# Sending the products of the recurrence's gates and of the pooling's groups as 272, 264 and 256 columns, with their sample sums joined

## The chip, the cores and the metric

The kernel runs on one core of a Trainium2 chip. Its engines work side by side and wait for each other only where one needs what another makes: PE multiplies matrices into accumulators, DVE and ACT do elementwise work (ACT also the sigmoids and exponentials), POOL does a little more of it, and SP starts the transfers. Every engine takes its instructions in the order in which they are written. The metric is the time of one execution on the device, in microseconds (us).

## The reference

One layer of a decoder is computed for 256 prompt tokens and 8 sample tokens (264 columns in the kernel), in float32 with a model width of 2048:

```python
xn = rms_norm(x, g_mix)
z = xn @ w_in                       # u_pool 512 | u_lru 1024 | u_gel 1024 | c_a 512 | c_b 512
y_pool = pool_mixer(u_pool, ...)    # trailing means less the token, then 4 blocks 128x128, a scale
xc = causal_dwconv(u_lru, 4 taps)
gate_r = sigmoid(xc_block @ w_a + b_a)      # 8 blocks of 128x128
gate_i = sigmoid(xc_block @ w_x + b_x)      # 8 blocks of 128x128
a = exp(-8 * gate_r * softplus(-lam))
h = scan(a, xc * gate_i * sqrt(1 - a*a))
y_lru = (h * gelu(u_gel)) @ w_lru_br
y_conf = silu(layer_norm(causal_dwconv(c_a * sigmoid(c_b), 31 taps))) @ w_conf_br
x = x + (sum of sigmoid(xn @ w_gate + b_gate) * (y_pool @ w_pool_br, y_lru, y_conf)) @ w_out
x = x + square(relu(rms_norm(x, g_mlp) @ w_up)) @ w_down
y = rms_norm(x, g_final)
```

The states of the convolutions, of the pooling and of the recurrence come back as further outputs. The change touches the sixteen products that make `gate_r` and `gate_i`, and the four 128x128 products of the pooling's groups.

## The kernel before, in words

The work lies transposed: channels on the 128 partitions, the 264 tokens in the columns. Each float32 number is held as two parts in a shorter format, a high part (the number rounded) and a low part (the rest). A product is the sum of three: high weight times high token, low weight times high token, high weight times low token; low times low is left out. Tokens lie in memory as low part (columns 0 to 263) and then high part (264 to 527), each with the 256 prompt tokens ahead of the 8 samples.

There are two forms of the three products, in `mm3` and `mm` (from line 238):

```python
ALIKE = (False, N, 2 * N), (True, N, 2 * N), (False, 0, N)
MIXED = (False, TP, 2 * N), (True, N, 2 * N), (False, 0, TP)
```

ALIKE sends 264 columns three times, and all land on the accumulator's columns 8 to 271. MIXED sends 272 columns (the low parts of the 8 samples and all high parts, which lie side by side), 264, and 256 (the low parts of the prompt). Both are 792 columns. In MIXED the low parts of the samples land apart, in columns 0 to 7, and have to be added to the samples' columns afterwards. `join` (lines 159 to 166) does that: one engine, ACT or DVE, copies the 8 columns to a small tile `side`, and DVE adds them to the accumulator. The dense products use MIXED, and `join` (or an addition in their evacuation) follows them at the end of each group. The sixteen gate products and the four pooling products use ALIKE and need no join.

The weights come as a stream of chunks, 1024 columns wide (eight 128x128 blocks, 24 matmuls, each with its weight load) or 512 for the gates and the groups (12 matmuls). For each chunk ACT rounds it to its high part `whi` (line 222) and DVE takes the difference for the low part `wlo` (line 223). There are four buffers for each, and the split of the chunk three places ahead is written out ahead of the matmuls of the chunk at hand. Eight chunks make a dense group of four accumulators; there are eight accumulators in all (`bufs=8`), so an open group leaves four free.

The gate products stand in four chunks of 512 columns, called gate blocks one to four below, put behind chunks 1, 3, 5 and 6 of the dense group w_in 4 (`LRU_AT`, line 55). So between blocks one and two, and two and three, stand two dense chunks, between three and four one, and behind block four the last chunk of that group; then the next group (w_in 6) opens with four accumulators. Each block makes two channel tiles of two gates, in the four accumulators that the open group leaves free. ACT reads each with a sigmoid (lines 525 and 526), and with that the accumulator is free for the next block, or for the next group. The pooling's groups take one such chunk in the middle of group w_gate 0; ACT reads their four accumulators at line 779.

The order on each engine is that of the main loop (from line 1008): in each turn the split of the chunk three ahead, the matmuls, the evacuation of a finished group, then the background work of the three mixers as far as a planner's credits allow: for DVE here the pooling's running sums (line 745) and differences (lines 757 to 762), and the product with the second gate (line 530). Those instructions stay in that order on the chip, whatever is ready.

Of the kernel before, what the change touches and what calls it, by code (L numbers as in the profile page):

```python
# [92 lines left out]
def hybrid_step(ctx: ExitStack, tc: tile.TileContext, first, par_in, st_in, wall, y_out, st_out):  # L93
# [17 lines left out]
    L = cpool.tile([P, 8 * PITCH], F32R, name="L", tag="L")  # L111
# [10 lines left out]
    def pv(name, i=None, n=1):  # L122
        a, b = PCOL[name]
        return par[:, a:b] if i is None else par[:, a + i:a + i + n]

    def part(t, k, a, n):
        at = k * PITCH + SKEW + a
        return t[:, at:at + n]
# [7 lines left out]
    def both(t, k):  # L136
        return part(t, k, 0, 2 * N)
# [4 lines left out]
    def lows(t, k):  # L142
        return two_of(t, k, 0)

    def highs(t, k):
        return two_of(t, k, N)
# [4 lines left out]
    def acc():  # L151
        return psum.tile([P, 512], F32, name="acc", tag="acc")

    def tokens(ps):
        return ps[:, TS:TS + N]
# [3 lines left out]
    def join(ps, by_act):  # L159
        t = side[:, len(joined) % 4, :]  # L160
        joined.append(t)
        if by_act:
            nc.scalar.copy(t, ps[:, :TS])
        else:
            nc.vector.tensor_copy(t, ps[:, :TS])
        nc.vector.tensor_tensor(ps[:, N:N + TS], ps[:, N:N + TS], t, op=ALU.add)
# [71 lines left out]
    ALIKE = (False, N, 2 * N), (True, N, 2 * N), (False, 0, N)  # L238
    MIXED = (False, TP, 2 * N), (True, N, 2 * N), (False, 0, TP)
# [6 lines left out]
    def mm(ps, hi, lo, x, what, start, stop=False):  # L246
        low_w, a, b = what
        o = TS + N - (b - a) if b > N else TS
        nc.tensor.matmul(ps[:, o:o + b - a], lo if low_w else hi, x[:, a:b], start=start, stop=stop,  # L249
                         skip_group_check=True)  # L250

    def mm3(ps, hi, lo, x, first, last, form):
        for k in range(3):
            mm(ps, hi, lo, x, form[k], first and k == 0, last and k == 2)
# [16 lines left out]
    def mark(q, flag):  # L271
        stage(q, "none", 0.0, [lambda: done.add(flag)], 0)

    def later(n, fn):
        delayed.append((now[0] + n, fn))
# [26 lines left out]
    def spend(**kw):  # L302
        for e, c in kw.items():
            credit[e] -= c
# [205 lines left out]
    def stage_split(q, n, hi, lo, x, gap=1):  # L510

        stage(q, "act", 0.65, [lambda i=i: nc.scalar.copy(hi(i), x(i)) for i in range(n)])
        stage(q, "dve", 0.71, [lambda i=i: nc.vector.tensor_tensor(lo(i), x(i), f(hi(i)), op=ALU.subtract)
                               for i in range(n)], gap)

    def lru_gate_mm(ct, c, j):
        assert "xc" in done
        hi, lo = whi[:, c % NHI, :], wlo[:, c % NHI, :]
        out = []
        for t in range(2):  # L520
            s = slice((2 * j + t) * P, (2 * j + t + 1) * P)
            ps = acc()
            mm3(ps, hi[:, s], lo[:, s], both(L, ct), True, True, ALIKE)
            out.append(ps)
        nc.scalar.activation(RA[:, ct, :], tokens(out[0]), AF.Sigmoid, bias=pv("b_lru_a", ct))
        nc.scalar.activation(TM[:, ct, :], tokens(out[1]), AF.Sigmoid, bias=pv("b_lru_x", ct))
        spend(act=1.0)
        if ct % 2:
            def times():
                nc.vector.tensor_tensor(XC[:, ct - 1:ct + 1, :], XC[:, ct - 1:ct + 1, :], TM[:, ct - 1:ct + 1, :],  # L530
                                        op=ALU.mult)
                spend(dve=0.71)

            later(1, times)
# [198 lines left out]
    def Q():  # L733
        if not q_at:
            q_at.append(cpool.tile([P, 8 * PITCH], F32R, name="Q", tag="Q"))
        return q_at[0]
# [35 lines left out]
    def grp_mm(c):  # L772
        assert "pool" in done
        hi, lo = whi[:, c % NHI, :], wlo[:, c % NHI, :]
        for gi in range(4):
            s = slice(gi * P, (gi + 1) * P)
            ps = acc()
            mm3(ps, hi[:, s], lo[:, s], both(Q(), gi), True, True, ALIKE)
            nc.scalar.activation(DU[:, gi, :], tokens(ps), AF.Copy, scale=pv("pool_scale", gi))
        stage_split("pool", 2, lambda c: highs(Q(), 2 * c), lambda c: lows(Q(), 2 * c), lambda c: DU[:, 2 * c:2 * c + 2, :])  # L780
        mark("pool", "grp")
# [226 lines left out]
    for i, ch in enumerate(chunks):  # L1008
# [18 lines left out]
        kind, gi, c, _ = ch  # L1027
# [26 lines left out]
        elif kind == "lru":  # L1054
            for j in range(2):
                lru_gate_mm(2 * gi + j, i, j)
            if gi == 3:
                lru_tail()
        elif kind == "grp":
            grp_mm(i)  # L1060
# [198 lines left out]
```

## Time and profile before

| | us |
|---|---|
| median of three runs (lowest, highest) | 1372.77 (1372.33, 1373.48) |
| the profiled execution | 1372.8 |
| its span on the core | 1370.9 |
| PE busy | 1365.0 |
| DVE busy | 894.3 |
| ACT busy | 729.4 |
| gate blocks one to four on PE | 102.5 to 122.6 |
| pooling's groups on PE | 182.6 to 184.0 |

A row of the timeline gives start, duration, engine, line and operation, the tile written and the tiles read, the shape, how many were merged into the row, and in brackets how long the engine stood idle ahead of it and for whom. Durations of neighbours on one engine overlap by about a tenth of a microsecond, since an instruction starts while the one ahead of it is still writing; so a place in a queue is priced by the distance of two starts.

### The profile page before, as it was taken

The page shows a single profiled execution, that of the slowest core. Times are in us where ns is not written, and L with a number is a line of the kernel's source. Part 1 is how long each engine was busy: PE and PEld are TensorE (multiplying, and loading weights), DVE is VectorE, ACT ScalarE, POOL GpSimd, SP SyncE. Part 2 cuts the span into 40 slices and gives each one's busy share as a digit, 9 for nine tenths or more (in the row PEclk, how much of TensorE's full clock was granted, in tenths as well). Part 3 has the DMA queues.
Part 4 walks back from the last instruction along what each step waited for, and adds up shares of the span by engine and source line. Part 5 has one row for each costly group of instructions (what it writes and reads, how often), then busy time and mean ns, then how long its engine had stood idle before and what let it go on. Part 6 is the DMA issues. An engine that isn't in the chain of part 4 may idle for free.

```text
span 1370.9 us, 27000 instructions
## 1 busy us (share of the span) xinstructions
PE 1365.0 (100%) x11459; PEld 1363.4 (99%) x11459; DVE 894.3 (65%) x1470; ACT 729.4 (53%) x1067; POOL 88.0 (6%) x122
## 2 busy tenths in 40 slices
PE   9999999999999999999999999999999999999998
PEld 9999999999999999999999999999999999999998
DVE  8777888876877669666656455655465645465644
ACT  7667677657664646455544334543344533354544
POOL 0300010110102014011000000000000000000112
PEclk9999999999999999999999999999999999999999
DMA  8655555555565555555555555555555555555552
GB/s 322 213 188 188 182 192 192 184 182 189 186 209 191 183 185 173 197 182 184 189 185 185 185 185 185 186 184 185 184 186 185 185 185 185 185 186 185 183 187 85
DMA packets 40968, 257.51 MB, mean 188 GB/s; under 512 B 4496, under 2 KB 6672, under 8 KB 11920
## 3 DMA queue, kind: packets, MB, share of 16 engines
q1 hardware_dynamic: 40704, 255.67, 55.0%
q8 instruction: 89, 1.46, 0.4%
q14 instruction: 31, 0.25, 0.1%
q10 hardware_dynamic: 144, 0.13, 0.0%
HBM read 252.57 MB, written 3.21 MB: 187 GB/s over the span
## 4 chain that ended last, share of the span: by engine, by line
PE 99%; DVE 0%; issue 0%; DVEq 0%
PE acc L249 99%; PE acc L346 0%; DVE y L1119 0%; DVE G L1114 0%; DVE X L900 0%; PE acc L329 0%; DVE G L1131 0%; DVE y L1153 0%; DVE G L902 0%; DVE G L1110 0%; DVE G L1113 0%; DVE X L911 0%; DVE X L906 0%; DVE G L1112 0%; DVEq L1153 0%
## 5 line engine op out<-in xcount | busy, mean ns | idle before, releaser
L223 DVE TENSOR_TENSOR wlo<-raw,whi 128x1024 fp32r<-128x1024 f32 (+1 forms) x478 | 581.5, 1219 | 435.2 <-ACT whi L222 434.6
L222 ACT CAST whi<-raw 128x1024 fp32r<-128x1024 f32 (+1 forms) x478 | 496.9, 1042 | 568.7 <-PE acc L249 500.5
L249 PE MATMUL acc<-A,whi 128*128 128x272 f32 (+2 forms) x3968 | 708.1, 282 | 0.0
L249 PEld LDWEIGHTS acc<-A,whi 128*128 128x128 f32 x3968 | 609.2, 188 | 0.5 <-ACT whi L232 0.5
L249 PE MATMUL acc<-A,wlo 128*128 128x264 f32 x1984 | 555.7, 282 | 0.0
L249 PEld LDWEIGHTS acc<-A,wlo 128*128 128x128 f32 x1984 | 371.0, 188 | 0.0
L249 PE MATMUL acc<-xn,whi 128*128 128x272 f32 (+1 forms) x2048 | 365.6, 281 | 0.0
L249 PEld LDWEIGHTS acc<-xn,whi 128*128 128x128 f32 x2048 | 314.6, 188 | 0.0
L249 PE MATMUL acc<-xn,wlo 128*128 128x264 f32 x1024 | 288.7, 282 | 0.0
L249 PEld LDWEIGHTS acc<-xn,wlo 128*128 128x128 f32 x1024 | 192.3, 188 | 0.0
L249 PE MATMUL acc<-Q,whi 128*128 128x256 f32 (+2 forms) x776 | 140.7, 281 | 0.0
L249 PE MATMUL acc<-LH,whi 128*128 128x272 f32 (+1 forms) x768 | 138.7, 281 | 0.0
L249 PEld LDWEIGHTS acc<-Q,whi 128*128 128x128 f32 x776 | 120.1, 188 | 0.0
L249 PEld LDWEIGHTS acc<-LH,whi 128*128 128x128 f32 x768 | 118.6, 188 | 0.0
L249 PE MATMUL acc<-Q,wlo 128*128 128x264 f32 x388 | 109.5, 282 | 0.0
L249 PE MATMUL acc<-LH,wlo 128*128 128x264 f32 x384 | 108.2, 282 | 0.0
L249 PEld LDWEIGHTS acc<-Q,wlo 128*128 128x128 f32 x388 | 72.9, 188 | 0.0
L249 PEld LDWEIGHTS acc<-LH,wlo 128*128 128x128 f32 x384 | 72.1, 188 | 0.0
L646 ACT ACTIVATE G<-tmp,par 128x256 f32<-128x256 f32 x120 | 54.4, 500 | 8.4 <-DVE G L649 7.5
L924 POOL TENSOR_SCALAR G<-G 128x264 f32<-128x264 f32 x1 | 0.4, 418 | 656.8 <-ACT G L866 656.8
L649 DVE TENSOR_TENSOR G<-G 128x1024 f32<-128x1024 f32 x30 | 38.2, 1274 | 0.0
L914 DVE TENSOR_TENSOR X<-X,acc 128x264 f32<-128x264 f32 x79 | 33.5, 424 | 6.4 <-PE acc L249 6.4
(193 smaller groups left out, 622.9 us busy)
## 6 DMA issues: line engine op xcount, KB each, us to landing
raw<-wall_dram SPq DMA_DIRECT2D x226, 1024.0 KB, 4.9
raw<-wall_dram SPq DMA_DIRECT2D x12, 512.0 KB, 6.1
raw<-first_dram SPq DMA_DIRECT2D x6, 512.0 KB, 8.2
y_dram<-y SPq DMA_DIRECT2D x7, 256.0 KB, 2.4
X<-first_dram SPq DMA_DIRECT2D x6, 264.0 KB, 7.9
raw<-wall_dram SPq DMA_DIRECT2D x5, 256.0 KB, 3.2
tmp<-first_dram SPq DMA_DIRECT2D x3, 388.0 KB, 5.0
tmp<-st_dram SPq DMA_DIRECT2D x4, 188.0 KB, 5.1
```

Of the source, the lines that this page charges most:

```text
L222: nc.scalar.copy(h[:, s], r[:, s])
L223: nc.vector.tensor_tensor(lo[:, s], r[:, s], f(h[:, s]), op=ALU.subtract)
L249: nc.tensor.matmul(ps[:, o:o + b - a], lo if low_w else hi, x[:, a:b], start=start, stop=stop, skip_group_check=True)
L646: nc.scalar.activation(dst[:, ct, :TP], vext[:, ct, k:k + TP], AF.Copy, scale=par[:, w:w + 1])
L649: nc.vector.tensor_tensor(VC[:, :, :TP], VC[:, :, :TP], src[:, :, :TP], op=ALU.add)
L914: nc.vector.tensor_tensor(X[:, m, :], X[:, m, :], tokens(whole), op=ALU.add)
L924: nc.gpsimd.tensor_scalar(sq2, sq2, 1.0, EPS * D / P, op0=ALU.mult, op1=ALU.add)
```

## The change

The gate products and the pooling's products take the form MIXED, and each is followed at once by `join`. In a pair of gates the first is copied by ACT and the second by DVE; of the four pooling groups, 0 and 2 by ACT and 1 and 3 by DVE. No matmul is added or taken away.

```diff
@@ lru_gate_mm
         for t in range(2):
             s = slice((2 * j + t) * P, (2 * j + t + 1) * P)
             ps = acc()
-            mm3(ps, hi[:, s], lo[:, s], both(L, ct), True, True, ALIKE)
+            mm3(ps, hi[:, s], lo[:, s], both(L, ct), True, True, MIXED)
+            join(ps, t == 0)
             out.append(ps)
         nc.scalar.activation(RA[:, ct, :], tokens(out[0]), AF.Sigmoid, bias=pv("b_lru_a", ct))
         nc.scalar.activation(TM[:, ct, :], tokens(out[1]), AF.Sigmoid, bias=pv("b_lru_x", ct))
@@ grp_mm
-            mm3(ps, hi[:, s], lo[:, s], both(Q(), gi), True, True, ALIKE)
+            mm3(ps, hi[:, s], lo[:, s], both(Q(), gi), True, True, MIXED)
+            join(ps, gi % 2 == 0)
             nc.scalar.activation(DU[:, gi, :], tokens(ps), AF.Copy, scale=pv("pool_scale", gi))
```

Three places show what it does to the order. The first is DVE's queue around gate block four, before: `L223` are splits of weight chunks, `L530` multiplies by the second gate, `L513` splits the pooling's differences, and `acc_1224` belongs to the dense group that ends there.

```order
L223 TENSOR_TENSOR wlo_65<-raw_63,whi_64 128x1024 x2
L530 TENSOR_TENSOR G_76<-G_76,tmp0_69 128x528
L513 TENSOR_TENSOR Q_1482<-G_76,Q_1482 128x2x264 x2
L223 TENSOR_TENSOR wlo_65<-raw_63,whi_64 128x1024 x2
L166 TENSOR_TENSOR acc_1224<-acc_1224,side_83 128x8
```

The same queue now, with the accumulators 1541 to 1561 of gate block four:

```order
L223 TENSOR_TENSOR wlo_65<-raw_63,whi_64 128x1024
L531 TENSOR_TENSOR G_76<-G_76,tmp0_69 128x528
L513 TENSOR_TENSOR Q_1506<-G_76,Q_1506 128x2x264 x2
L223 TENSOR_TENSOR wlo_65<-raw_63,whi_64 128x1024
L166 TENSOR_TENSOR acc_1541<-acc_1541,side_83 128x8
L165 COPY side_83<-acc_1547 128x8
L166 TENSOR_TENSOR acc_1547<-acc_1547,side_83 128x8
L166 TENSOR_TENSOR acc_1555<-acc_1555,side_83 128x8
L165 COPY side_83<-acc_1561 128x8
L166 TENSOR_TENSOR acc_1561<-acc_1561,side_83 128x8
L223 TENSOR_TENSOR wlo_65<-raw_63,whi_64 128x1024
L166 TENSOR_TENSOR acc_1224<-acc_1224,side_83 128x8
```

DVE, which had no part in the gates' accumulators, now has six small instructions there (four additions, two copies), behind two splits of weight chunks and the other work of those turns.

The second place is ACT's queue at the same block, before (`L546` is the tanh that opens the recurrence's tail):

```order
L512 CAST Q_1482<-G_76 128x2x264 x2
L222 CAST whi_64<-raw_63 128x1024 x2
L525 ACTIVATE tmp2_71<-acc_1517,par_66 128x264
L526 ACTIVATE tmp0_69<-acc_1521,par_66 128x264
L525 ACTIVATE tmp2_71<-acc_1527,par_66 128x264
L526 ACTIVATE tmp0_69<-acc_1531,par_66 128x264
L546 ACTIVATE tmp0_69<-tmp2_71,sp_81 128x264 x3
```

And now:

```order
L512 CAST Q_1506<-G_76 128x2x264 x2
L222 CAST whi_64<-raw_63 128x1024 x2
L163 COPY side_83<-acc_1541 128x8
L526 ACTIVATE tmp2_71<-acc_1541,par_66 128x264
L527 ACTIVATE tmp0_69<-acc_1547,par_66 128x264
L163 COPY side_83<-acc_1555 128x8
L526 ACTIVATE tmp2_71<-acc_1555,par_66 128x264
L527 ACTIVATE tmp0_69<-acc_1561,par_66 128x264
L547 ACTIVATE tmp0_69<-tmp2_71,sp_81 128x264 x3
```

Ahead of each pair of sigmoids stands a copy, and the second pair's copy stands behind the first pair's sigmoids. Each sigmoid now reads what DVE's addition has written.

The third place is PE's queue where the next dense group (w_in 6) opens, now, with what each matmul waits for:

```order
L249 MATMUL acc_1227<-A_68,whi_64 128x256
L249 MATMUL acc_1617<-A_68,whi_64 128x272 [waits Activation_49]
L249 MATMUL acc_1617<-A_68,wlo_65 128x264
L249 MATMUL acc_1617<-A_68,whi_64 128x256
L249 MATMUL acc_1618<-A_68,whi_64 128x272 [waits Activation_49]
L249 MATMUL acc_1618<-A_68,wlo_65 128x264
L249 MATMUL acc_1618<-A_68,whi_64 128x256
L249 MATMUL acc_1619<-A_68,whi_64 128x272 [waits Activation_49]
```

These accumulators are the places of block four's, 1541 to 1561, in the same order, and the waits for ACT are for its sigmoids; before, the same four places were handed on in the same way. Gate blocks two to four take the places of the block ahead of them.

## The prediction

> **What bounds the kernel now.** I read the page's busy shares and its chain of waits, then the stretch of the gate blocks by windows, then the timeline of each engine there.
>
> ```profile
> span 1370.9 us, 27000 instructions
> PE 1365.0 (100%) x11459; PEld 1363.4 (99%) x11459; DVE 894.3 (65%) x1470; ACT 729.4 (53%) x1067; POOL 88.0 (6%) x122
> ...
> PE 99%; DVE 0%; issue 0%; DVEq 0%
> ```
>
> PE never pauses and is 99% of the chain that ends last. So every time at which PE has to wait is added to the end, and work elsewhere costs nothing until PE waits for it. The stretch of the four gate blocks (engines in the order PE, PEld, DVE, ACT, POOL):
>
> ```profile
> 102.50:126.00 23.50, 23.50 (x199) 23.50 (x198) 19.24 (x39) 17.01 (x31) 0.00 (x0) 1.00 0.57 189
> ```
>
> PE has no gap there, and DVE is busy for 19.24 of 23.50 us (82%), against 65% over the span: it is the engine with the least room, and the one that the change adds to. PE's places:
>
> ```profile
> 121.19 0.28 PE L249 MATMUL acc<-L,whi 128*128 128x264 f32 x1
> ...
> 122.65 0.28 PE L249 MATMUL acc<-A,whi 128*128 128x272 f32 x1
> ...
> 125.39 0.41 PE L249 MATMUL acc<-A,whi 128*128 128x256 f32 x2
> ...
> 189.63 0.41 PE L249 MATMUL acc<-A,whi 128*128 128x256 f32 x2
> ```
>
> Block four starts at 121.19, the last dense chunk at 122.65. The second of the two matmuls merged at 125.39 opens the next dense group, at 125.51. At 189.63 the second likewise opens the second chunk behind the pooling's groups (189.75).
>
> **What the columns are worth.** Both forms send 792 columns for a product. Twelve ALIKE matmuls take 122.65 - 121.19 = 1.46 us, 0.1217 each; 24 MIXED ones take 125.51 - 122.65 = 2.86, 0.1192 each. Sixty matmuls change: at most 60 x 0.0025 = 0.15 gained; I take -0.13. The Trainium skill, TensorE: Matmul & The Clock Gate, section Back-to-back issue gap, gives for matmuls in a row a fixed cost and a rate per column, by which three matmuls of 792 columns cost the same however they are cut; the sum by it would be 0.13 higher. The rows differ from it slightly, and they decide.
>
> **What a join costs where it stands.** Twenty additions and ten copies go to DVE, ten copies to ACT:
>
> ```profile
> L163 ACT COPY side<-acc 128x8 f32<-128x8 f32 x44 | 6.7, 170 | 12.4 <-PE acc L249 12.4
> ...
> 127.38 0.17 DVE L166 TENSOR_TENSOR acc<-acc,side 128x8 f32<-128x8 f32 x1
> 127.58 0.43 DVE L596 TENSOR_TENSOR tmp<-acc,rstd 128x264 f32<-128x264 f32 x1
> ```
>
> And ACT's rows at the blocks, where before DVE had no part:
>
> ```profile
> 103.24 0.48 ACT L525 ACTIVATE tmp<-acc,par 128x264 f32<-128x264 f32 x1
> ...
> 104.70 1.07 ACT L222 CAST whi<-raw 128x1024 fp32r<-128x1024 f32 x1
> ...
> 119.48 1.18 ACT L512 CAST Q<-G 128x528 fp32r<-128x528 f32 x2
> 120.54 2.02 ACT L222 CAST whi<-raw 128x1024 fp32r<-128x1024 f32 x2
> ...
> 123.53 0.52 ACT L526 ACTIVATE tmp<-acc,par 128x264 f32<-128x264 f32 x1
> 123.90 1.37 ACT L546 ACTIVATE tmp<-tmp,sp 128x264 f32<-128x264 f32 x3
> 125.12 1.09 ACT L222 CAST whi<-raw 128x1024 fp32r<-128x1024 f32 x1
> ...
> 130.37 0.92 ACT L546 ACTIVATE tmp<-tmp,sp 128x264 f32<-128x264 f32 x2 [1.74 <-DVE G L530]
> ```
>
> An addition holds up what depends on it for 0.20 (127.38 to 127.58), so a hand-off is 0.03 beyond its 0.17; where the next instruction doesn't depend on it, it takes 0.10 of the queue (neighbours overlap by some 0.08). What matters is the zigzag in a block, counted from DVE's first addition: ACT's first sigmoid starts at 0.20, its second 0.365 later (a quarter of 104.70 - 103.24), its second copy at 0.93 and ends at 1.10; DVE's third addition can start at 1.13, and DVE is through at 1.53. ACT's third sigmoid starts at 1.33, and ACT is through at 2.06. Before, ACT was through in 1.46.
>
> ACT frees block four's accumulators by 123.53 + 0.52 = 124.05, 1.46 ahead of the group that takes them at 125.51. Now its sigmoids wait for DVE's place in its queue. DVE's rows:
>
> ```profile
> 104.89 0.99 DVE L745 TENSOR_TENSOR qtmp<-qtmp 128x804 f32<-128x804 f32 x1
> 105.80 1.23 DVE L223 TENSOR_TENSOR wlo<-raw,whi 128x1024 fp32r<-128x1024 f32 x1
> ...
> 110.25 0.40 DVE L757 SCALAR_TENSOR_TENSOR G<-qtmp 128x240 f32<-128x240 f32 x1
> ...
> 111.98 0.17 DVE L762 SCALAR_TENSOR_TENSOR G<-G,tmp 128x8 f32<-128x8 f32 x1
> 112.82 1.23 DVE L223 TENSOR_TENSOR wlo<-raw,whi 128x1024 fp32r<-128x1024 f32 x1 [0.67 <-ACT whi L222]
> ...
> 117.07 0.17 DVE L762 SCALAR_TENSOR_TENSOR G<-G,tmp 128x8 f32<-128x8 f32 x1
> 118.15 1.23 DVE L223 TENSOR_TENSOR wlo<-raw,whi 128x1024 fp32r<-128x1024 f32 x1 [0.91 <-ACT whi L222]
> 121.64 1.23 DVE L223 TENSOR_TENSOR wlo<-raw,whi 128x1024 fp32r<-128x1024 f32 x1 [2.27 <-ACT whi L222]
> ...
> 124.64 1.22 DVE L223 TENSOR_TENSOR wlo<-raw,whi 128x1024 fp32r<-128x1024 f32 x1
> 126.24 1.22 DVE L223 TENSOR_TENSOR wlo<-raw,whi 128x1024 fp32r<-128x1024 f32 x1 [0.38 <-ACT whi L222]
> ...
> 129.57 0.70 DVE L530 TENSOR_TENSOR G<-G,tmp 128x528 f32<-128x528 f32 x1
> ...
> 134.09 1.23 DVE L223 TENSOR_TENSOR wlo<-raw,whi 128x1024 fp32r<-128x1024 f32 x1 [2.69 <-ACT whi L222]
> ```
>
> In its queue the block stands ahead of the rows at 104.89, 110.25, 119.29 (118.15 + 1.14) and 125.78 (124.64 + 1.14).
>
> **The walk.** *Block one*: DVE is there at 104.89, through at 106.42; ACT through at 106.95 (before 104.70). PE waits for nothing yet. *Block two*: ACT's cast ends at 106.95 + 1.07 = 108.02, and DVE's split behind it starts at 108.04; from there to the block take 110.25 - 105.80 = 4.45, so DVE is there at 112.49, ACT through at 114.55. *Block three*: DVE goes on at 114.02; two pooling differences (111.98 + 0.10 - 110.25 = 1.83) bring it to 115.85; from the split to the last difference take 117.07 + 0.10 - 112.82 = 4.35, then a split of 1.14: it is there at 121.34, 2.05 behind 119.29. Its first sigmoid ends at 121.34 + 0.20 + 0.48 = 122.02, and block four on PE, due at 121.19, starts at 122.05: **0.86**. Its third accumulator comes at 121.34 + 1.33 + 0.48 + 0.03 = 123.18 against 122.78: **0.40**. *Block four*: ACT is through block three at 123.40; its two casts of the pooling (1.06) and the next weight cast (1.07) end at 125.53; DVE's split starts at 125.55, and from 121.64 to 125.78 it is 4.14: there at 129.69. The first accumulator is free at 129.69 + 0.20 + 0.48 + 0.03 = 130.40. PE, with 1.26 lost so far, would open the next group at 126.77: **3.63**. The third accumulator comes at 131.53 against 131.12: **0.41**. So the walk loses 5.30 up to here.
>
> *Behind it*: ACT is through at 131.75; three tanh (1.22) and a cast (1.07) later, DVE's split starts at 134.06, 7.82 behind 126.24. The chain from there to the split at 134.09 is serial (product L530, tanh, a table load, exponential, cast, split); that split ended at 135.32 for a matmul due at 125.51 + 4 x 2.865 + 0.12 = 137.09, so had 1.77 to spare, and now is 7.82 - 5.30 = 2.52 later against PE: **0.75**. The next splits gain on PE, and the lag is gone.
>
> *The pooling's groups*: the same zigzag.
>
> ```profile
> 185.00 1.27 DVE L571 TENSOR_TENSOR_SCAN tmp<-tmp,tmp 128x256 f32<-128x256 f32 x2
> ...
> 185.19 1.19 ACT L512 CAST Q<-G 128x528 fp32r<-128x528 f32 x2
> ...
> 187.35 1.23 DVE L223 TENSOR_TENSOR wlo<-raw,whi 128x1024 fp32r<-128x1024 f32 x1 [1.09 <-ACT whi L222]
> ```
>
> DVE is there at 185.00, ACT through at 187.06 instead of 185.19; the split at 187.35, which hangs on ACT, starts 1.87 later and ends at 190.45; its matmul is due at 189.75 + 0.12 = 189.87: **0.58**. The accumulators are not wanted soon here.
>
> Sum: 0.86 + 0.40 + 3.63 + 0.41 + 0.75 + 0.58 - 0.13 = 6.5. The profiled execution took 1372.8 (the median is 1372.77): **1379.3**.
>
> Bounds: with a hand-off of 0.10, as from 129.57 + 0.70 to 130.37, instead of 0.03, the same walk loses some 3 us more, since each step of the zigzag, each split behind its cast and each accumulator handed to PE hangs on one: 1382.3. With none, and DVE's small steps at their shortest, about 1.5 less: 1377.8. Below that the lag would have to pile up less than the rows say.
>
> **Rivals.** *The lag doesn't pile up.* If DVE made up each block's loss in its idle times (0.67, 0.91, 2.27 and 0.38 in the rows above), it would be at block four at 125.78 as before, the first accumulator free at 126.49: 0.98, with the third 1.4, less the columns: 1374.1. Against it: those idle times are waits for ACT's casts, and ACT is late itself by the sigmoids.
>
> *PE slows down after the long wait.* At the start PE is slower:
>
> ```profile
> 0.77 3.79 PE L346 MATMUL acc<-const-bfloat16-1.0 128*128 128x256 bf16 x17 [0.77 <-PEq L1231]
> 4.57 1.77 PE L249 MATMUL acc<-A,whi 128*128 128x264 f32 x8
> 6.18 0.64 PE L249 MATMUL acc<-A,wlo 128*128 128x264 f32 x4
> ```
>
> Seventeen matmuls in 3.80 (0.22 each), eight in 1.61 (0.20), then four in 0.48 (0.12). If a wait of 3.6 put PE back there for some 5 us, it would lose 5 x (1 - 0.12/0.22) = 2.3: 1381.6. The Trainium skill, TensorE: Matmul & The Clock Gate, section What's actually happening, names an idle window of about 3.4 us, free-running; by it a wait barely longer seldom covers one whole. The start agrees in kind; no wait in this trace is long enough to show the rest.
>
> *Not slower.* If DVE reached block four 0.7 ahead of 125.51, at 124.8, all joins would lie beside PE's work, and the columns' 0.13 would remain: 1372.7. That is its deciding point, and even before the change DVE is there only at 125.78; it would have to take its instructions out of order. That the form doesn't change is excluded by PE's rows in the order.
>
> **Chances.** The piled lag (1376.5 to 1381.0) 0.70, longer hand-offs or a slower PE (above 1381) 0.15, no pile-up 0.10, not slower 0.05. A change within 0.2% (2.75 us) can't be told from none: slower 0.85, same 0.13 (the third case and most of the last), faster 0.02 (should the last bring more than the columns). The range leaves out the last two cases and the far end: 1375.8 to 1382.5.
>
> **What would show it.** PE's first gaps: at block four (about 1.3 in two parts), a wait of about 3.6 at the next group's first matmul put down to ACT's sigmoids, and half a microsecond behind each of 136 and 189. ACT's sigmoids should wait for DVE's additions, 2 to 4 us at blocks two to four. If PE's waits are short and DVE reaches block four by 126, the piling was wrong; if matmuls of 0.2 follow the long wait, the clock rival holds.

## The result, and the profile after

The changed kernel takes 1380.59 us (median of five runs, 1379.63 to 1381.34), against 1372.77 before: 1.0055 times as long, with a 95% interval from 1.0044 to 1.0067. So it is slower by 7.8 us, and the forecast of 1379.3 (1375.8 to 1382.5) was 1.3 too low. The profiled execution is the shortest of the five, 1379.63, with a span of 1377.8, which is 6.9 above the span before. The five spans run from 1377.7 to 1379.5 with 1378.0 in the middle, and the time around the span differs from run to run (1.8 to 2.9 us); so what a trace can show is a little more than 7 us.

The page's busy shares, and the shares of its chain of waits:

```profile
span 1377.8 us, 27050 instructions
...
PE 1366.8 (99%) x11459; PEld 1364.5 (99%) x11459; DVE 897.7 (65%) x1500; ACT 730.2 (53%) x1077; POOL 88.1 (6%) x122
...
PE 96%; DVE 2%; ACT 1%; issue 0%; DMA 0%; DVEq 0%; ACTq 0%
```

There are as many matmuls as before (11459), and 40 instructions more on DVE and ACT. The chain that ends last no longer stays on PE: it passes through DVE and ACT for about 3% of the span. PE's waits, with their sum, their number and the longest:

```profile
PE acc L249 <- ACT tmp L526: 4.1, 2, 3.3
...
PE acc L249 <- DVE wlo L223: 0.5, 1, 0.5
```

Before, this view had no wait of PE behind the start. Now the stretch of the gate blocks that was full before, and the ten microseconds after it (PE, PEld, DVE, ACT, POOL, the granted clock, DMA share, GB/s):

```profile
102.50:126.00 23.50, 22.56 (x187) 22.14 (x186) 17.58 (x53) 14.62 (x29) 0.00 (x0) 1.00 0.57 186
126.00:136.00 10.00, 6.71 (x45) 6.50 (x44) 6.37 (x16) 6.41 (x19) 0.00 (x0) 0.83 0.31 105
```

In the second row stands something that the sum had not: a granted clock of 0.83. PE's timeline shows the places:

```profile
120.72 0.28 PE L249 MATMUL acc<-A,whi 128*128 128x256 f32 x1
121.79 0.39 PE L249 MATMUL acc<-L,whi 128*128 128x272 f32 x1 [0.80 <-ACT tmp L526]
122.02 0.28 PE L249 MATMUL acc<-L,wlo 128*128 128x264 f32 x1
...
122.52 0.82 PE L249 MATMUL acc<-L,whi 128*128 128x256 f32 x2
123.17 0.29 PE L249 MATMUL acc<-L,wlo 128*128 128x264 f32 x1
...
126.60 0.28 PE L249 MATMUL acc<-A,whi 128*128 128x256 f32 x1
130.16 0.59 PE L249 MATMUL acc<-A,whi 128*128 128x272 f32 x1 [3.29 <-ACT tmp L526]
130.56 0.42 PE L249 MATMUL acc<-A,wlo 128*128 128x264 f32 x1
...
133.36 0.40 PE L249 MATMUL acc<-A,whi 128*128 128x256 f32 x2
...
195.78 0.41 PE L249 MATMUL acc<-A,whi 128*128 128x256 f32 x2
196.71 0.39 PE L249 MATMUL acc<-A,wlo 128*128 128x264 f32 x1 [0.53 <-DVE wlo L223]
```

A loss is the distance of two starts less 0.12 for each matmul between them (the number in brackets is shorter, since a matmul still runs for a while behind its start). Ahead of block four PE loses 121.79 - 120.72 - 0.12 = 0.95, and 0.11 more because the first matmul after a wait takes 0.23 (121.79 to 122.02); inside the block, at its third accumulator, 0.41 (122.52 to 123.17 for two matmuls); at the next group's opening 3.44 (126.60 to 130.16). Then fourteen matmuls take 133.36 - 130.16 = 3.20 instead of 1.67: 1.53 lost. At the pooling's groups it is 0.69 (195.78 to 196.71 for two matmuls) and again a restart of about 0.10. Together 7.23; less the 0.13 of the columns 7.10. PE's last dense matmul starts at 1367.00 instead of 1360.01, which is 6.99 later; this execution is 0.24 us ahead of the one before where the first gate block starts (102.29 against 102.53), so from there on PE loses 7.23. These five places hold the loss to within 0.2 us.

DVE's queue at the four blocks, with the waits of its third addition in the last:

```profile
104.65 0.17 DVE L166 TENSOR_TENSOR acc<-acc,side 128x8 f32<-128x8 f32 x1
...
112.28 0.17 DVE L166 TENSOR_TENSOR acc<-acc,side 128x8 f32<-128x8 f32 x1
...
121.06 0.17 DVE L166 TENSOR_TENSOR acc<-acc,side 128x8 f32<-128x8 f32 x1
...
129.43 0.17 DVE L166 TENSOR_TENSOR acc<-acc,side 128x8 f32<-128x8 f32 x1
...
130.57 0.17 DVE L166 TENSOR_TENSOR acc<-acc,side 128x8 f32<-128x8 f32 x1 [0.70 <-ACT side L163]
```

With the 0.24 us by which this execution is ahead at the first block, in the old count DVE is there at 104.89, 112.52, 121.30 and 129.67. ACT's rows at blocks two to four and behind:

```profile
112.48 0.48 ACT L526 ACTIVATE tmp<-acc,par 128x264 f32<-128x264 f32 x1 [2.28 <-DVE acc L166]
...
121.26 0.48 ACT L526 ACTIVATE tmp<-acc,par 128x264 f32<-128x264 f32 x1 [3.07 <-DVE acc L166]
...
129.63 0.48 ACT L526 ACTIVATE tmp<-acc,par 128x264 f32<-128x264 f32 x1 [3.35 <-DVE acc L166]
130.01 0.47 ACT L527 ACTIVATE tmp<-acc,par 128x264 f32<-128x264 f32 x1
130.37 0.17 ACT L163 COPY side<-acc 128x8 f32<-128x8 f32 x1
130.78 0.48 ACT L526 ACTIVATE tmp<-acc,par 128x264 f32<-128x264 f32 x1 [0.24 <-DVE acc L166]
```

Before, ACT's sigmoids there waited for PE's product or stood behind ACT's own casts, and never waited for DVE. The first of block two, before:

```profile
110.26 0.48 ACT L525 ACTIVATE tmp<-acc,par 128x264 f32<-128x264 f32 x1 [1.17 <-PE acc L249]
```

Now the first sigmoid of each of these blocks waits 2.3 to 3.4 us for DVE's place in its queue, and behind it the second pair's copy and sigmoids form the zigzag: DVE waits 0.70 for ACT's copy, ACT waits 0.24 for DVE's addition.

### The profile page after: what moved, and what is told of

Read it like the earlier page. It is cut to its first block, busy times and chain, and to the rows that moved or that the text cites. A ratio compares the mean times of both kernels' runs of the same rounds, so it can differ in the third digit from the quotient of the medians.

```text
span 1377.8 us, 27050 instructions
## 1 busy us (share of the span) xinstructions
PE 1366.8 (99%) x11459; PEld 1364.5 (99%) x11459; DVE 897.7 (65%) x1500; ACT 730.2 (53%) x1077; POOL 88.1 (6%) x122
## 3 DMA queue, kind: packets, MB, share of 16 engines
q8 instruction: 89, 1.46, 0.4%
## 4 chain that ended last, share of the span: by engine, by line
PE 96%; DVE 2%; ACT 1%; issue 0%; DMA 0%; DVEq 0%; ACTq 0%
PE acc L249 96%; DVE wlo L223 1%; ACT whi L222 0%; DMA tmp<-first_dram 0%; DVE y L1121 0%; DVE qtmp L746 0%; ACT Q L512 0%; DVE L L513 0%; ACT tmp L526 0%; DVE G L531 0%; DVE acc L166 0%; ACT G L781 0%; ACT tmp L527 0%; DVE tmp L597 0%; DVE G L758 0%
## 5 line engine op out<-in xcount | busy, mean ns | idle before, releaser
L223 DVE TENSOR_TENSOR wlo<-raw,whi 128x1024 fp32r<-128x1024 f32 (+1 forms) x478 | 581.4, 1219 | 435.1 <-ACT whi L222 434.5
L249 PE MATMUL acc<-Q,whi 128*128 128x272 f32 (+1 forms) x776 | 140.7, 281 | 0.0
L166 DVE TENSOR_TENSOR acc<-acc,side 128x8 f32<-128x8 f32 x208 | 35.9, 173 | 10.4 <-ACT side L163 5.1
```

The lines of the kernel that those rows point to most:

```text
L223: nc.vector.tensor_tensor(lo[:, s], r[:, s], f(h[:, s]), op=ALU.subtract)
```

## The experiments

Each was measured beside runs of the kernel before on the same chip, which gave 1372.8 to 1372.9. The theory is the prediction's: the joins tie the gates' accumulators to DVE's place in its queue, DVE and ACT fall behind block by block, and PE waits for the accumulators.

### The two places of the change apart

First the gates alone, with the pooling's products as before:

```diff
-            mm3(ps, hi[:, s], lo[:, s], both(Q(), gi), True, True, MIXED)
-            join(ps, gi % 2 == 0)
+            mm3(ps, hi[:, s], lo[:, s], both(Q(), gi), True, True, ALIKE)
```

> Only the gates take the new form and its joins; the pooling's groups stay as they were. Theory (joins stand late in DVE's queue and hold the accumulators that PE wants): the wait behind the groups, 0.69 in the trace after, goes and the rest stays: about 1379.9. Rival (each of the twenty joins has a price of its own, 7.8 / 20 = 0.39): 1380.6 - 4 x 0.39 = 1379.0.

Measured: 1379.59 (1379.02 to 1380.34), 1.0049 [1.0037, 1.0062]. Then the pooling's groups alone, with the gates as before:

```diff
-            mm3(ps, hi[:, s], lo[:, s], both(L, ct), True, True, MIXED)
-            join(ps, t == 0)
+            mm3(ps, hi[:, s], lo[:, s], both(L, ct), True, True, ALIKE)
```

> Only the pooling's groups take the new form. Theory: one wait of PE of 0.6 to 0.7 for a low part, the clock stays full: 1373.4. Rival (a price for each join): 1372.8 + 4 x 0.39 = 1374.4.

Measured: 1373.64 (1373.22 to 1374.39), 1.0006 [0.9997, 1.0015]. In its timeline PE has one wait, at the second chunk behind the groups:

```profile
190.30 0.39 PE L249 MATMUL acc<-A,wlo 128*128 128x264 f32 x1 [0.52 <-DVE wlo L223]
```

The gates cost 6.8, the groups 0.8, together 7.6 of the 7.8. In the traces the two add up less simply. From the first gate block to the last dense matmul PE loses 6.93 with the gates alone, against 7.23 in the changed kernel. Behind the long wait twenty matmuls take 4.39 us with the gates alone (130.43 to 134.82), 2.01 too much instead of 1.53, since the clock falls later there and the wait at the third accumulator isn't covered. The price of the groups, one zigzag that delays one split, comes alone just as it does beside the gates; its time taken alone can't be told from none, but its row in the trace can. A price for each join (1379.0 and 1374.4) can't be excluded by these two times; it falls with the earlier blocks below, where as many joins cost half as much.

### The columns without the joins, and the joins without the dependence

Two kernels cut the change the other way. In the first the products send 272, 264 and 256 columns and nothing is joined:

```diff
             mm3(ps, hi[:, s], lo[:, s], both(L, ct), True, True, MIXED)
-            join(ps, t == 0)
...
             mm3(ps, hi[:, s], lo[:, s], both(Q(), gi), True, True, MIXED)
-            join(ps, gi % 2 == 0)
```

> The gates and the groups send 272, 264 and 256 columns, but the 8 sample columns of low parts are not added (that part of the samples' result is left out). Theory: no wait of PE is left, and only the columns' gain of 0.13 stands: 1372.7. Rival (the form itself costs, by its columns or its place in the accumulator): well above 1373, up to 1380.

Measured: 1372.42 (1372.03 to 1373.23), 0.9997 [0.9988, 1.0006], and no wait of PE. The second is the kernel before with as many small instructions on ACT and DVE, at the same places of the program, on a tile in memory, not on the accumulators, that nobody waits for:

```diff
+    aside = side
+    def idle(by_act):
+        if by_act:
+            nc.scalar.copy(aside[:, 0, :], eps.to_broadcast([P, TS]))
+        else:
+            nc.vector.tensor_copy(aside[:, 1, :], eps.to_broadcast([P, TS]))
+        nc.vector.tensor_tensor(aside[:, 2, :], aside[:, 2, :], eps.to_broadcast([P, TS]), op=ALU.add)
...
             mm3(ps, hi[:, s], lo[:, s], both(L, ct), True, True, ALIKE)
+            idle(t == 0)
...
             mm3(ps, hi[:, s], lo[:, s], both(Q(), gi), True, True, ALIKE)
+            idle(gi % 2 == 0)
```

> The kernel before with the same twenty additions and ten copies on DVE and ten copies on ACT at the same places of the queues, but on a tile aside, so that no accumulator and no sigmoid waits for them. Theory: hidden, 1372.8. Rival (DVE's and ACT's added time is what costs): 1374 to 1378.

Measured: 1372.68 (1372.2 to 1373.78), 0.9999 [0.999, 1.0009]. PE has no wait behind the start here either. So neither the cut of the columns nor the work of the forty additions and copies costs anything that these times can show (to about 1.3 us). What costs is that they stand between PE's accumulators and the sigmoids that free them.

### DVE's other work ahead of the blocks

If the lag is DVE's, taking work off its queue in this stretch must shorten PE's waits. This kernel makes neither the pooling's running sums nor its differences:

```diff
+    nc.gpsimd.memset(G[:, 8:12, :], 0.0)
...
-        for i, cost in enumerate((1.2, 0.9, 0.6, 0.3)):
-            stage("pool", "dve", cost, [lambda i=i: add(i)])
...
-        stage("pool", "dve", 0.8, [lambda gi=gi: diff(gi) for gi in range(4)])
```

> As changed, without the pooling's running sums and differences on DVE (the pooling's result is left out: a constant stands in its place). Theory: DVE has some 7 us less ahead of the joins and reaches block four 3 us earlier against PE; the long wait falls from 3.4 to about 0.6, the clock stays full: 1375.1 (2.3 over its own kernel before). Rival (the zigzag of copies and additions between ACT and DVE is the price, wherever it stands): little changes, 1379 or more.

Measured: 1376.26 (1375.51 to 1377.02), 1.0025 [1.0016, 1.0034]. The same cut made in the kernel before:

> The kernel before without the same pooling work on DVE: the control of the run without that work. All theories: PE has no wait there to lose: 1372.8.

Measured: 1372.72 (1372.49 to 1373.58), 1.0 [0.999, 1.0009]. The cut work was worth nothing before the change, and 4.3 us after it. PE's waits that are left in the first of the two (beside one at the groups and a short one at an accumulator):

```profile
125.85 0.39 PE L249 MATMUL acc<-A,whi 128*128 128x272 f32 x1 [0.54 <-ACT tmp L527]
...
138.98 0.39 PE L249 MATMUL acc<-A,wlo 128*128 128x264 f32 x1 [0.87 <-DVE wlo L223]
```

The wait at the next group's opening falls from 3.44 to 0.70, and those at block four go; at the third accumulator of that group 0.42 is lost (126.57 to 127.23 for two matmuls). The time came out 1.2 above the expectation, which names no price for the split of the fifth chunk of that group, where PE loses 1.03 and a restart of 0.11. With the groups the rows add up to 3.0; the median is 3.5 above the kernel before on that chip. The run also moves something: the cast and the split of the pooling's differences (1.17 us on ACT, 1.32 on DVE), which stand ahead of block four in the changed kernel, come around block one here. So it takes that work out of block four's way too.

### The slow matmuls behind the long wait

The fourteen slow matmuls stand in a stretch with half the clock. The two windows around its start, in the changed kernel:

```profile
126.45:129.86 3.41, 0.43 (x4) 0.21 (x2) 3.38 (x8) 0.23 (x1) 0.00 (x0) 1.00 0.00 0
129.86:133.28 3.42, 3.12 (x14) 3.12 (x15) 0.42 (x4) 3.18 (x9) 0.00 (x0) 0.50 0.81 266
```

I chose the bounds so that all of the half clock lies in the second row: it lasts 3.42 us. To see whether the clock is the cause of the slow matmuls, and what it costs in the end, 33 matmuls were put ahead of the long wait. They write columns that nobody reads, in accumulators whose group is finished:

```diff
+FILL = 33
...
+            if c == n - 1 and (name, groups[gi][3]) == ("w_in", 4):
+                for k in range(FILL):
+                    nc.tensor.matmul(pss[k % 4][:, 272:512], whi[:, i % NHI, :P], both(a_all, k % 4)[:, :240],
+                                     start=False, stop=False, skip_group_check=True)
             if c == n - 1:
                 for m in range(4):
```

> As changed, with 33 matmuls of 240 columns put on PE behind the last chunk ahead of the long wait; they write unused columns of the accumulators just finished and count for nothing. Theory with the clock: the wait stays for the same sigmoids, but PE is busy in it, the granted clock stays 1.00, and the 1.4 lost to half rate behind it goes, while up to 0.75 comes back as a wait at the fifth chunk of that group: 1379.2 to 1379.9. Rival (the slow matmuls behind the wait are a start-up of PE's queue and not the clock): 1380.6 or more, with slow matmuls still there.

Measured: 1380.32 (1380.1 to 1380.55), 1.0054 [1.0041, 1.0067]. The window and PE's timeline:

```profile
126.00:136.00 10.00, 9.91 (x86) 9.71 (x84) 6.37 (x16) 6.40 (x19) 0.00 (x0) 1.00 0.31 107
```
```profile
126.79 3.86 PE L1050 MATMUL acc<-A,whi 128*128 128x240 f32 x33
130.49 0.29 PE L250 MATMUL acc<-A,whi 128*128 128x272 f32 x1
...
131.10 0.76 PE L250 MATMUL acc<-A,whi 128*128 128x256 f32 x2
131.70 0.29 PE L250 MATMUL acc<-A,wlo 128*128 128x264 f32 x1
...
143.04 0.39 PE L250 MATMUL acc<-A,wlo 128*128 128x264 f32 x1 [0.46 <-DVE wlo L224]
```

The clock stays at 1.00 and the matmuls behind the fill take 0.12 each: the idle time is what brought the clock down. The fill takes the pause away together with the slow clock, so it can't by itself exclude a slow start of PE behind a pause. The kernel with the gates alone can:

```profile
130.43 0.39 PE L249 MATMUL acc<-A,whi 128*128 128x272 f32 x1 [3.29 <-ACT tmp L526]
...
131.16 1.01 PE L249 MATMUL acc<-A,whi 128*128 128x256 f32 x2
131.97 0.42 PE L249 MATMUL acc<-A,wlo 128*128 128x264 f32 x1
```

There the first five matmuls behind the same wait take 0.73 us, 0.23 and then 0.12 each, and the slow ones begin only when the granted clock falls, at 131.37.

With the fill the total doesn't fall, and there my expectation (1379.2 to 1379.9) missed. Two waits that the slow matmuls had covered are back: 0.36 at the third accumulator (131.10 to 131.70 for two matmuls), and 0.61 with a restart of 0.11 at the fifth chunk's split (143.04), which in the changed kernel PE reached too late to have to wait. Some 0.2 more is the fill's own: PE opens the group at 130.49, while the accumulator was free at about 130.29 (ACT's sigmoid there runs from 129.78 to 130.26). PE's last dense matmul starts at 1366.93, against 1367.00 without the fill.

### The last blocks one chunk earlier

With blocks three and four behind chunks 4 and 5, one more dense chunk lies between block four and the next group:

```diff
-LRU_AT = ((4, 1), (4, 3), (4, 5), (4, 6))
+LRU_AT = ((4, 1), (4, 3), (4, 4), (4, 5))
```

> As changed, with gate blocks three and four one chunk earlier, so that two dense chunks (5.7 us) instead of one stand between block four and the group that takes its accumulators; the count of joins is the same. Theory: the long wait is gone, block three or four loses 1.5 to 2 and the groups 0.6: about 1375.4, clock full. Rival (a price for each join): as changed, 1380.6.

Measured: 1376.7 (1374.97 to 1377.81), 1.0025 [1.0016, 1.0034]. And the kernel before with the same edit:

> The kernel before with gate blocks three and four one chunk earlier. If moving the blocks costs nothing by itself: 1372.8, no wait of PE. Rival: the move itself brings waits, and part of what the two kernels with earlier blocks cost is the move's: 1374 or more.

Measured: 1372.64 (1372.07 to 1373.62), 0.9998 [0.9988, 1.0007]. So the move costs nothing by itself, and in the changed kernel it saves some 4 us, since the long wait goes. What is left in the profiled execution is a wait at block four (1.65 by its starts, and 0.41 at its third accumulator), and again half the clock behind it:

```profile
119.68 0.40 PE L249 MATMUL acc<-L,whi 128*128 128x272 f32 x1 [1.49 <-ACT tmp L526]
```
```profile
118.00:121.36 3.36, 1.72 (x12) 1.33 (x11) 2.53 (x11) 1.97 (x6) 0.00 (x0) 1.00 0.65 273
121.36:124.78 3.42, 3.42 (x18) 3.42 (x18) 2.67 (x4) 2.80 (x5) 0.00 (x0) 0.50 0.20 31
```

That the clock stays up was my expectation, and it fell: it came down although PE was busy for half of the 3.36 us ahead. It doesn't do so each time, as far as the mean clock of a run tells (only one run has a trace). Of the ten runs four show a mean clock of 0.998 and spans of 1374.7 to 1375.4; the other six show 1.0, five of them with spans of 1373.2 to 1373.8 (the sixth has 1375.8, for which I have no reason). The stretch of half clock is worth about 1.5.

### The zigzag

Last the order inside a block: all four products and joins first, then the four sigmoids:

```diff
+    held4 = []
...
         for t in range(2):
...
             join(ps, t == 0)
-            out.append(ps)
-        nc.scalar.activation(RA[:, ct, :], tokens(out[0]), AF.Sigmoid, bias=pv("b_lru_a", ct))
-        nc.scalar.activation(TM[:, ct, :], tokens(out[1]), AF.Sigmoid, bias=pv("b_lru_x", ct))
+            held4.append(ps)
+        if j == 0:
+            return
+        for k in range(2):
+            nc.scalar.activation(RA[:, ct - 1 + k, :], tokens(held4[2 * k]), AF.Sigmoid, bias=pv("b_lru_a", ct - 1 + k))
+            nc.scalar.activation(TM[:, ct - 1 + k, :], tokens(held4[2 * k + 1]), AF.Sigmoid, bias=pv("b_lru_x", ct - 1 + k))
...
```

> The four products of a gate block with their joins come first, then the four sigmoids: no copy of ACT stands behind a sigmoid any more, so DVE's six small instructions run through without waiting for ACT, and ACT's copies run ahead of DVE's place in its queue. If the zigzag between ACT and DVE is what makes DVE and ACT lose time inside each block, the two waits ahead of and inside block four (0.95 and 0.41 in the changed kernel) go. DVE still comes to block four some 4 us after its place before, so the wait at the next group's first matmul stays at about 3.5, with half the clock for 3.4 us behind it (about 1.4): 3.6 + 1.4 + 0.7 at the pooling's groups + some 0.2 of restarts = about 1378.5, 2.1 below the changed kernel. Rival: DVE's lag alone makes the waits, and the zigzag only adds to what is hidden: 1380.5 as the changed kernel, with the waits at block four still there.

Measured: 1379.56 (1379.11 to 1380.95), 1.0049 [1.0031, 1.0067]. The runs overlap with those of the changed kernel, so the time alone doesn't tell the two apart; the rows do. PE's and DVE's:

```profile
121.31 0.28 PE L249 MATMUL acc<-A,whi 128*128 128x256 f32 x1
121.61 0.39 PE L249 MATMUL acc<-L,whi 128*128 128x272 f32 x1
...
129.58 0.59 PE L249 MATMUL acc<-A,whi 128*128 128x272 f32 x1 [3.29 <-ACT tmp L530]
```
```profile
128.84 0.17 DVE L166 TENSOR_TENSOR acc<-acc,side 128x8 f32<-128x8 f32 x1
128.92 0.15 DVE L165 COPY side<-acc 128x8 f32<-128x8 f32 x1
129.11 0.25 DVE L166 TENSOR_TENSOR acc<-acc,side 128x8 f32<-128x8 f32 x2
...
129.45 0.17 DVE L166 TENSOR_TENSOR acc<-acc,side 128x8 f32<-128x8 f32 x1
```

DVE runs through a block without a wait (0.8 from its first addition to its last end, instead of 1.6), PE loses 0.18 and a restart of 0.11 ahead of block four instead of 0.95 and 0.11, and nothing inside it. The long wait stays at 3.45, and the sixteen matmuls behind it, all but the last at half the clock, lose 1.63. By these rows this kernel loses 0.29 + 3.45 + 1.63 + 0.79 - 0.13 = 6.0, which makes 1378.8; the median is 0.8 above that, and these rows don't show where. So the zigzag makes the waits at block four, and the lag of DVE makes the long one.

Both repairs together, the order without the zigzag and the earlier blocks:

> The same, and gate blocks three and four stand one chunk earlier, so that a dense chunk lies between block four and the opening of the next group twice over. If the lag of DVE against PE is all that costs, a wait of about 0.5 is left at block four and one of 0.7 at the pooling's groups, no wait is long enough to bring the clock down, and the time is about 1374.2. Rival: the clock falls also behind waits of this size, as it did in half the runs behind 1.7 us: 1375.6. If the zigzag didn't matter: 1375.2 to 1376.7, as with the earlier blocks alone.

Measured: 1374.55 (1373.75 to 1375.56), 1.0011 [1.0001, 1.002]. The granted clock stays at 1.00 around the blocks, and PE's waits are the two expected:

```profile
118.54 0.40 PE L249 MATMUL acc<-L,whi 128*128 128x272 f32 x1 [0.47 <-ACT tmp L530]
...
190.83 0.39 PE L249 MATMUL acc<-A,wlo 128*128 128x264 f32 x1 [0.53 <-DVE wlo L223]
```

They lose 0.62 and 0.68, and a restart of 0.11 each: 1.5, less the columns 1.4; the measured difference on this chip is 1.7. This wins back 6 of the 7.8 us, but it doesn't beat the kernel before. Since PE had no wait there to lose, a version with the joins could win at most the columns' 0.13; that is an argument, and no run shows it.

## Why the prediction was right, and where it was off

**PE is the bound, and each wait of it is added to the end.** Right: the losses read off PE's rows add up to 7.10, and from the first gate block to its last dense matmul it loses 7.23.

**The columns, -0.13.** The kernel without joins came out at 0.9997 [0.9988, 1.0006] of before. That time agrees with 0.13 less and with nothing, but its trace shows the gain: the four gate blocks and the groups take 1.43, 1.43, 1.42, 1.42 and 1.43 us on PE, where before they took 1.45 and four times 1.46, together 0.16 less. The formula of equal price, in the Trainium skill, TensorE: Matmul & The Clock Gate, section Back-to-back issue gap, is given there for an isolated matmul, without a share for its weight load. Here each of the 11459 matmuls has one.

**The walk.** DVE was to reach the blocks at 104.89, 112.49, 121.34 and 129.69; it came, in the same count, at 104.89, 112.52, 121.30 and 129.67. The pile-up was worked out from rows of the kernel before alone, where none of these waits existed, and it holds to 0.04 us. The reason that I gave for it also held: DVE's idle times between the blocks couldn't take up the lag, since they are waits for ACT's casts, and ACT was late by its sigmoids (DVE's split behind block three starts at 125.30 after 2.65 of waiting). The step that decides the bounds, a hand-off of 0.03 instead of 0.10, held as well: ACT's sigmoid at 129.63 starts 0.03 behind the end of the addition at 129.43, and DVE's addition at 130.57 starts 0.03 behind the end of ACT's copy at 130.37.

**The waits of PE.** Forecast 0.86, 0.40 and 3.63 at block four, its third accumulator and the next group's opening; measured 0.95, 0.41 and 3.44. At the groups 0.58 against 0.69. The restart of 0.1 behind a wait, in which the first matmul takes 0.23, was not in my sum, and it is there at every wait at full clock.

**The term of 0.75 at the fifth chunk and the 0.41 ahead of it.** These two don't appear in the changed kernel, and their reason was nevertheless right: with the fill they are there at 0.72 and 0.36. What took their place is the rival that I had put beside the main case instead of into it.

**The rival of the slow PE.** This step was wrong. I let "a wait barely longer seldom covers one whole" decide, and put the slow clock together with longer hand-offs at 0.15. It came in the changed kernel, with the gates alone and without the zigzag, behind waits of 3.3; and in four of ten runs behind one of 1.5. It was also mis-sized: I took 5 us of slow matmuls and 2.3, and it lasted 3.42 us and cost 1.53 with the restart. That it did little harm to the forecast was luck: two costs stood in a row and one covered the other. While PE ran slowly, DVE and ACT caught up, and the 1.16 of the terms behind it went. Taking the slow clock away, as the fill did, left PE's end where it was (1366.93 against 1367.00). The start of the kernel, from which I took the size, doesn't show the same thing: its matmuls take 0.20 to 0.22 while its windows give a granted clock of 1.00, so what slows them there stays open.

The rule that I had weighed speaks of the same thing. The Trainium skill, TensorE: Matmul & The Clock Gate, section What's actually happening, names a free-running window of about 3.4 us, and that the clock goes down after an idle one. The length agrees with the trace: half the clock lasts 3.42 us. That the window is free-running agrees too: with the gates alone the clock falls not during the wait but 0.94 us after PE has resumed, as its windows show:

```profile
127.96:131.37 3.41, 0.94 (x6) 0.80 (x6) 2.55 (x9) 1.24 (x4) 0.00 (x0) 1.00 0.27 38
131.37:134.78 3.41, 3.27 (x15) 3.20 (x15) 0.71 (x1) 3.41 (x12) 0.00 (x0) 0.50 0.64 269
```

That the window has to be idle differs. In the 3.4 us ahead of the fall PE was busy for 0.43 us in the changed kernel, 0.94 with the gates alone, and 1.72 of 3.36 with the earlier blocks. These rows fit a clock that goes down where PE was busy for about half of a window or less. No run here varied that share by itself, so the bound is not shown; that a wholly idle window isn't needed is.

**The lag doesn't pile up; not slower.** Both fell with DVE's places. The deciding point of the last, DVE at block four by 124.8, was missed by 4.9. The first rival's sum also left out the 0.58 of the groups, which doesn't hang on the piling: it should have read about 1374.6.

**The size.** 6.5 was forecast, and the rows give 7.1: 0.37 more for the slow matmuls (1.53) than for the two terms they replaced (1.16), 0.21 for the restarts at block four and at the groups, 0.21 more at the small waits, and 0.19 less at the long one. The median lies another 0.7 higher, since the run that is the median has a span of 1377.7 and spent 2.9 us around it, where the profiled execution of before spent 1.9.

## What to carry to other kernels

A few tenths of a microsecond of work on an engine with room are free only as long as nothing waits for them: here forty small instructions cost nothing that could be measured when no one needed them, and 7.8 us when they stood between an accumulator and the engine that frees it, because then the whole queue ahead of them is part of the way. Before a step is given to a second engine, look up where that engine's queue stands at this moment, walk the lag through every round in which the buffers come back, and put independent small steps ahead of those that wait for another engine. And where the bound engine will wait for a microsecond and more, reckon with slower work behind it, but look also at what that slowness covers.

## What was unexpected in the hardware

PE's granted clock was halved for 3.42 us also where PE had been busy for 1.72 of the 3.36 us ahead, and, by the mean clock, in four of ten runs of one and the same kernel. The first matmul behind a wait for another engine held PE for 0.23 us instead of 0.12, with the clock at 1.00.
